# A hybrid decoder step on one core: matmul rows and split weights at other addresses modulo 256

## The chip, the core and the metric

The kernel runs on one core of a Trainium2 chip, as one program. The metric is the device time of one execution in microseconds (us), taken as the median of several. TensorE (PE) multiplies, PEld stands for its weight loads, VectorE (DVE), ScalarE (ACT) and GpSimd (POOL) do the elementwise work, and SyncE (SP) issues most of the DMAs.

## What is computed

One inference step of a two-layer decoder with 256 prompt tokens and 8 sequences of 4 new tokens, 288 tokens in all, of width 1024. Each layer is a mixer between two half-step SwiGLU FFNs. Cut to what matters here:

```python
def swiglu(x, w_gu, w_down):                       # w_gu 1024 x 5632, w_down 2816 x 1024
    g, u = jnp.split(x @ w_gu, 2, axis=-1)
    return (jax.nn.silu(g) * u) @ w_down

for i in range(2):
    x = x + 0.5 * swiglu(rmsnorm(x, norm_ffa[i]), w_ffa_gu[i], w_ffa_down[i])
    h = rmsnorm(x, norm_mix[i])
    x = x + (short_conv_mixer(h, ...) if i == 0 else nsa(h, ...))   # each with an input and an output projection
    x = x + 0.5 * swiglu(rmsnorm(x, norm_ffb[i]), w_ffb_gu[i], w_ffb_down[i])
y = rmsnorm(x, norm_final)
```

All weights and activations are fp32. The attention mixer (nsa) reads a compressed, a selected and a windowed cache.

## The kernel before

Activations lie transposed: channels on the 128 partitions, the 288 tokens along the row. A weight matrix comes in chunks of up to 1 MB from HBM (Weights.load_ahead, L209) into a ring of four buffers, raw. A unit is half a chunk: up to 8 blocks of 128 x 128. Each unit is split into two fp32r parts: ScalarE writes the rounded part, whi (L242), VectorE the remainder, wlo = raw - whi (L251). Both lie in the pool split, four buffers of 4096 bytes per partition for each name, all of whi first and then all of wlo. Activations are split in the same way into pairs of tiles: xh and xl hold the normed inputs (L395, L398), Ah and Al the products of gate and up, or of the convolution (L560, L561, L635, L636), and zh and zl the normed input of the last FFN.

A product of a unit is three matmuls for each of its blocks k (product; the profile shows them all at L307, in the helper mm): whi with xh, whi with xl, wlo with xh. The activations' row is the moving operand (288 columns), the weights' block is the one that is loaded (128 columns). All accumulate in one PSUM bank, which VectorE then empties. The code says in Python which engine does what in which order; the conversions of the next units stand between the products, two units ahead.

Each pair tile is made by rows(): row n begins at SKIP[name] + n x ROW fp32 words in the tile, where ROW is 320 words (1280 bytes, of which 1152 are used), and BEHIND adds unused words after the last row. The pool gives the tiles their places in the order in which they are first asked for, so SKIP, BEHIND and the sizes decide at which address modulo 256 the rows begin. As ROW is five times 256 bytes, all rows of a tile begin at the same address modulo 256, and so do all blocks of 512 bytes in a unit. In the program before these are:

| | whi | wlo | xh, Ah, zh | xl, Al, zl | raw |
|---|---|---|---|---|---|
| address modulo 256 | 64 | 64 | 64 | 128 | 64 |
| distance of a row from whi | | | 0 | 64 | |
| distance of a row from wlo | | | 0 | 64 | |

In the attention mixer the split ring's buffers hold pages of the cache for a while (L1030, load_pages). [...]

Of the kernel before, what the change touches and what calls it, by code (L numbers as in the profile page):

```python
# [8 lines left out]
F32 = mybir.dt.float32  # L9
F32R = mybir.dt.float32r  # L10
# [6 lines left out]
P = 128  # L17
# [49 lines left out]

V_FFA, V_PE, V_MIX, V_FFB, V_FIN, V_CONV = 0, 16, 32, 48, 64, 72

ROW = 320  # L70
SKIP = dict(xh=0, xl=16, Ah=56, Al=16, zh=56, zl=16)
BEHIND = dict(xl=8, zl=56)


def weight_chunks():

    steps = [range(k * P, (k + 1) * P) for k in range(NF)]

    def ffn(name, layer, first=False):
        for f0, f1 in HALVES:  # L80
            cuts = list(range(f0, f1, 2)) + [f1]
            if first and not f0:
                cuts = [f0] + list(range(f0 + 1, f1, 2)) + [f1]
            for f, e in zip(cuts, cuts[1:]):
                for c in (0, FF):
                    yield f"w_{name}_gu", layer, steps[:KD], [range(c + f * P, c + e * P)]
            m = (f1 - f0) // 2
            for d in range(0, KD, 2):
                for i in range(2):
                    yield f"w_{name}_down", layer, steps[f0 + i * m:f0 + (i + 1) * m], [range(d * P, (d + 2) * P)]  # L90

    yield from ffn("ffa", 0, True)
    for d in range(0, KD, 2):
        for part in (1, 2, 0):
            yield "w_conv_in", 0, steps[:KD], [range(part * D + d * P, part * D + (d + 2) * P)]
    for d in range(0, KD, 2):
        yield "w_conv_out", 0, steps[:KD], [range(d * P, (d + 2) * P)]
    yield from ffn("ffb", 0)
    yield from ffn("ffa", 1)
    for t in range(6):  # L100
        yield "w_nsa_in", 0, steps[:KD], [range(D + t * 256, D + (t + 1) * 256)]
    yield "w_nsa_in", 0, steps[:KD], [range(D + 6 * 256, N_IN)]
    for pr in range(2):
        for gp in range(2):
            yield "w_nsa_in", 0, steps[:KD], [range((2 * pr + kp) * 256 + gp * P, (2 * pr + kp) * 256 + (gp + 1) * P) for kp in range(2)]

    heads = [[r for kp in range(2) for r in range(((pr * 2 + kp) * 4 + g) * HD, ((pr * 2 + kp) * 4 + g + 1) * HD)]
             for pr in range(2) for g in range(4)]
    for d in range(0, KD, 2):
        yield "w_nsa_out", 0, heads, [range(d * P, (d + 2) * P)]  # L110
    yield from ffn("ffb", 1)


class Task:


    def __init__(self, engine, takes, put, after=(), slots=(), uses=(), rank=0.0):
        self.engine, self.takes, self.put, self.after, self.slots, self.rank = engine, takes, put, after, slots, rank
        self.end = None
        for x in (*slots, *uses):  # L120
            x.users.append(self)
# [53 lines left out]
class Weights:  # L175
# [5 lines left out]
    def __init__(self, nc, raw, split, bufs, given):  # L181
        self.given, self.at, self.plan = given, dict.fromkeys(given, 0), weight_chunks()
        self.nc, self.raw, self.split, self.bufs = nc, raw, split, bufs
        self.chunks, self.units = [], []
        self.loaded = self.done = self.used = 0
        self.live = 0
        self.left = {}
        self.tiles, self.parts, self.halves = {}, {}, {}
        self.stop = None
        self.behind = None  # L190

    def chunk(self):

# [27 lines left out]
    def low_behind(self):  # L221
# [2 lines left out]
            self.low(n)  # L224
        self.behind = []

    def high(self):
        c, view = self.units[self.done]
        v = view(self.tiles[c])
        hi, lo = [self.split.tile([P, 1024], F32R, name=n) for n in ("whi", "wlo")]  # L230
        n = 1
        for x in v.shape[1:]:
            n *= x
        parts = []
        for t in (hi, lo):
            t = t[:, :n]
            if len(v.shape) == 4:
                t = t.rearrange("p (k a c) -> p k a c", a=v.shape[2], c=v.shape[3])
            else:
                t = t.rearrange("p (k c) -> p k c", c=v.shape[2])  # L240
            parts.append(t)
        self.nc.scalar.activation(parts[0], v, AF.Copy)  # L242
        nk = v.shape[1]
        self.halves[self.done] = c, v, parts
        self.parts[self.done] = [t[:, :n].rearrange("p (k c) -> p k c", k=nk) for t in (hi, lo)]
        self.done += 1
        return self.done - 1
# [28 lines left out]
def tile_step(ctx, tc, x_turned, vectors, state_turned, cmp_pages, sel_pages, cache_win, win_pages, page_table,  # L276
# [3 lines left out]
    nc = tc.nc  # L280
    const = ctx.enter_context(tc.tile_pool(name="const", bufs=1))
    raw = ctx.enter_context(tc.tile_pool(name="raw", bufs=RAW))
    split = ctx.enter_context(tc.tile_pool(name="split", bufs=SPLIT))
# [52 lines left out]
    def tr(out, in_):  # L336
# [4 lines left out]
    W = Weights(nc, raw, split, RAW, dict(  # L341
        w_ffa_gu=w_ffa_gu, w_ffa_down=w_ffa_down, w_ffb_gu=w_ffb_gu, w_ffb_down=w_ffb_down, w_conv_in=w_conv_in,
        w_conv_out=w_conv_out, w_nsa_in=w_nsa_in, w_nsa_out=w_nsa_out))
# [41 lines left out]
    def rows(pool, name, n, **k):  # L385

        t = pool.tile([P, SKIP[name] + n * ROW + BEHIND.get(name, 0)], F32R, name=name, **k)
        return t[:, SKIP[name]:][:, :n * ROW].rearrange("p (n c) -> p n c", c=ROW)[:, :, :N]

    xh, xl = rows(const, "xh", KD), rows(const, "xl", KD)  # L390
# [143 lines left out]
    def pair(work, name, n):  # L534
        return [rows(work, name + part, n, bufs=1) for part in "hl"]
# [300 lines left out]
    def nsa(at):  # L836
# [167 lines left out]
        def load_chunk(tiles, b, j):  # L1004

            vs = [t.rearrange("p (s c) -> p s c", c=512) for t in tiles]
            if j != "w":
                at_ = page_numbers(b * 16 + j * 4, 4)
            s0 = 0
            for v in vs:  # L1010
                m = v.shape[1]
                if j == "w":
                    nc.sync.dma_start(v, win_pages[4 * b + s0:4 * b + s0 + m].rearrange("s p c -> p s c"))
                else:
                    for s in range(m):
                        nc.sync.dma_start(v[:, s:s + 1], sel_pages[bass.ds(at_[s0 + s], 1)].rearrange("s p c -> p s c"))
                s0 += m
            return vs

        def load_pages():  # L1020
            while len(pages) + len(done) < len(order):
                n = len(pages) + len(done)
                ring = max(room, key=lambda r: room[r] if r != "split" or n < PAGES["until"] else 0)
                if not room[ring] or ring == "split" and n >= PAGES["until"]:
                    return
                i, j, b2 = key = order[len(pages) + len(done)]
                b = 2 * i + b2
                room[ring] -= 1
                if ring == "split":
                    t = [split.tile([P, 1024], F32R, name=n).bitcast(F32) for n in ("whi", "wlo")]  # L1030
                else:
                    t = [(raw if ring == "raw" else early).tile([P, 2048], F32, name=ring)]
                pages[key] = load_chunk(t, b, j)
                rings[key] = ring
            W.stop, W.bufs = None, room["raw"]
            W.load_ahead()
# [106 lines left out]
        def load_more(at):  # L1143
            n = len(pages) + len(done) + W.loaded - W.attention
            load_pages()
            for k in range(n, min(len(pages) + len(done) + W.loaded - W.attention, len(loads))):
                queue[0] = max(queue[0], at) + LOAD
                loads[k].end = queue[0] + LAND
# [36 lines left out]
        x = Slot("tr")  # L1185
# [103 lines left out]
        def sequences(i):  # L1289
# [34 lines left out]
            def best():  # L1324

                left, kept = [T(n, [P, 34]) for n in ("left", "kept")]
                nc.vector.tensor_reduce(sc[:, 1:31], t["rank"][:, 2:62].rearrange("p (n r) -> p n r", r=2), AX.X, OP.add)
                high = T("top", [P, 8])
                for src_, dst in ((sc, left), (left, kept)):
                    nc.vector.max(high, src_[:, 0:33])  # L1330
                    nc.vector.match_replace(dst[:, 0:33], high, src_[:, 0:33], NEG)
                t["mk"] = T("mk", [P, 32], F32, 2)
                ts(t["mk"], kept[:, 0:32], 0.0, NEG, op0=OP.is_ge, op1=OP.mult)
# [288 lines left out]
```

## Time and profile before

| | us |
|---|---|
| median of 3 runs | 1236.58 (1236.1 to 1237.55) |
| the profiled execution | 1236.77 |
| its span, first to last instruction | 1235.0 |
| PE busy in the span | 1218.2 (99%) |
| PEld busy | 1153.3 (93%) |
| DVE busy | 730.3 (59%) |
| ACT busy | 571.1 (46%) |
| POOL busy | 236.8 (19%) |

The mean granted TensorE clock is 0.997 of full speed. DMA moves 262 MB, 212 GB/s over the span. In the profile a busy time counts each engine's instructions; matmuls overlap in the pipeline, so that their durations are longer than the distance between their starts. A group line gives a line of the kernel, engine, operation, output and inputs, shapes, count, then busy us and mean ns of one, then the idle time before them and what ended it.

### The profile page before, as it was taken

Reading aid. Unit: us, or ns where it says so; the run is one execution under the profiler, and the core shown is the slowest. Engines: PE = TensorE matmul, PEld = TensorE weight load, DVE = VectorE, ACT = ScalarE, POOL = GpSimd, SP = SyncE. Lnnn points to the kernel's source line nnn. Section 1 sums busy time; section 2 is a strip of 40 time slices with the busy share of each in tenths; the row PEclk is TensorE's granted clock in tenths of the full one; section 3 lists DMA queues with packets and bytes.
Section 4 is the critical chain, followed back from the end, with each engine's and each line's share of the span. In section 5 each row is a group of like instructions: output and inputs, shape, how many; then the busy total and the mean of one; then the engine's idle time right before and its main releaser. Section 6 shows DMA issues by size and latency. Waiting matters only on the chain.

```text
span 1235.0 us, 25757 instructions
## 1 busy us (share of the span) xinstructions
PE 1218.2 (99%) x10047; PEld 1153.3 (93%) x10047; DVE 730.3 (59%) x1363; ACT 571.1 (46%) x1011; POOL 236.8 (19%) x237
## 2 busy tenths in 40 slices
PE   9999999999999999999999999999999999999997
PEld 8999999999999999999899999999866699999997
DVE  6663555666765545556564455676568566655654
ACT  6443344533544334345443344544377645443444
POOL 0260121231321101212120012130022222200211
PEclk9999999999999999999999999999999999999999
DMA  7764655756566466546573453596699857575532
GB/s 280 262 219 174 235 175 185 256 188 221 189 217 211 155 211 236 195 152 237 198 238 119 174 178 113 175 344 211 238 366 332 294 206 282 211 254 205 165 102 80
DMA packets 89066, 262.00 MB, mean 212 GB/s; under 512 B 9937, under 2 KB 43090, under 8 KB 73714
## 3 DMA queue, kind: packets, MB, share of 16 engines
q1 hardware_dynamic: 87922, 249.66, 57.6%
q0 software_dynamic: 256, 8.32, 1.8%
q10 hardware_dynamic: 768, 2.38, 0.5%
q8 instruction: 79, 1.29, 0.4%
q14 instruction: 41, 0.34, 0.1%
HBM read 257.31 MB, written 11.35 MB: 218 GB/s over the span
## 4 chain that ended last, share of the span: by engine, by line
PE 92%; ACT 3%; DVE 3%; DMA 2%; issue 1%; POOL 0%; SPq 0%; DVEq 0%; ACTq 0%
PE mm L307 83%; PE tr L307 5%; PE acc L307 3%; PE tr L338 1%; DMA early<-in_sel_pages_dram 1%; ACT S L1219 1%; DVE wlo L251 1%; DMA raw<-in_w_nsa_out_dram 0%; ACT L542 0%; ACT whi L242 0%; DMA raw<-in_w_ffa_gu_dram 0%; DVE xT L591 0%; ACT S L1375 0%; DVE S L1371 0%; ACT sq L404 0%
## 5 line engine op out<-in xcount | busy, mean ns | idle before, releaser
L251 DVE TENSOR_TENSOR wlo<-raw,whi 128x1024 fp32r<-128x1024 f32 (+2 forms) x361 | 411.9, 1155 | 93.4 <-ACT whi L242 91.1
L307 PE MATMUL mm<-xh,whi 128*128 128x288 f32 (+1 forms) x1480 | 436.5, 297 | 2.5 <-DVE xl L1484 1.1
L307 PE MATMUL mm<-xl,whi 128*128 128x288 f32 (+1 forms) x1480 | 432.4, 294 | 0.0
L307 PE MATMUL mm<-xh,wlo 128*128 128x288 f32 (+1 forms) x1480 | 428.7, 292 | 0.0
L242 ACT ACTIVATE whi<-raw 128x1024 fp32r<-128x1024 f32 (+2 forms) x365 | 343.2, 952 | 97.5 <-PE mm L307 86.1
L307 PEld LDWEIGHTS mm<-xh,whi 128*128 128x128 f32 (+1 forms) x1480 | 276.8, 188 | 7.9 <-issue 3.8
L307 PEld LDWEIGHTS mm<-xl,whi 128*128 128x128 f32 (+1 forms) x1480 | 277.0, 188 | 0.5 <-DVE xl L398 0.2
L307 PEld LDWEIGHTS mm<-xh,wlo 128*128 128x128 f32 (+1 forms) x1480 | 276.0, 187 | 0.4 <-DVE wlo L251 0.2
L307 PE MATMUL mm<-Ah,whi 128*128 128x288 f32 x768 | 226.4, 295 | 0.0
L307 PE MATMUL mm<-Ah,wlo 128*128 128x288 f32 x768 | 224.9, 293 | 1.3 <-DVE wlo L251 1.1
L307 PE MATMUL mm<-Al,whi 128*128 128x288 f32 x768 | 225.4, 294 | 0.0
L557 POOL TENSOR_TENSOR a<-s,t 128x288 f32<-128x288 f32 x80 | 104.8, 1310 | 514.9 <-DVE t L555 376.4
L307 PEld LDWEIGHTS mm<-Ah,wlo 128*128 128x128 f32 x768 | 144.2, 188 | 2.7 <-DVE wlo L251 2.7
L307 PEld LDWEIGHTS mm<-Ah,whi 128*128 128x128 f32 x768 | 144.0, 188 | 0.7 <-issue 0.4
L307 PEld LDWEIGHTS mm<-Al,whi 128*128 128x128 f32 x768 | 144.0, 188 | 0.0
L553 ACT ACTIVATE s<-t 128x288 f32<-128x288 f32 x88 | 39.1, 445 | 159.2 <-DVE t L551 159.1
L560 ACT ACTIVATE Ah<-a 128x288 fp32r<-128x288 f32 x88 | 39.1, 445 | 154.4 <-POOL a L557 141.7
L555 DVE TENSOR_TENSOR t<-mm,rB 128x288 f32<-128x288 f32 x88 | 40.2, 457 | 111.8 <-PE mm L307 111.6
L307 PE MATMUL mm<-zh,whi 128*128 128x288 f32 x352 | 103.5, 294 | 0.0
L307 PE MATMUL mm<-zl,whi 128*128 128x288 f32 x352 | 103.3, 294 | 0.0
L307 PE MATMUL mm<-zh,wlo 128*128 128x288 f32 x352 | 102.8, 292 | 0.0
L591 DVE SCALAR_TENSOR_TENSOR xT<-mm,xT 128x288 f32<-128x288 f32 x64 | 29.2, 456 | 86.1 <-PE mm L307 85.6
(291 smaller groups left out, 1173.4 us busy)
## 6 DMA issues: line engine op xcount, KB each, us to landing
raw<-in_w_ffb_gu_dram SPq DMA_DIRECT2D x44, 1024.0 KB, 5.1
raw<-in_w_ffa_gu_dram SPq DMA_DIRECT2D x42, 1024.0 KB, 5.4
cp<-in_cmp_pages_dram SPq DMA_DIRECT2D x256, 128.0 KB, 4.4
early<-in_sel_pages_dram SPq DMA_DIRECT2D x56, 256.0 KB, 5.4
raw<-in_w_ffa_down_dram SPq DMA_DIRECT2D x16, 768.0 KB, 4.6
raw<-in_w_conv_in_dram SPq DMA_DIRECT2D x12, 1024.0 KB, 5.0
raw<-in_w_ffb_down_dram SPq DMA_DIRECT2D x16, 768.0 KB, 5.6
raw<-in_sel_pages_dram SPq DMA_DIRECT2D x48, 256.0 KB, 5.1
```

Source lines behind the costliest of these rows:

```text
L242: self.nc.scalar.activation(parts[0], v, AF.Copy)
L251: (lower or self.nc.vector).tensor_sub(parts[1], v, parts[0])
L307: nc.tensor.matmul(out, lhsT, rhs, start=start, stop=stop, skip_group_check=True)
L338: nc.tensor.transpose(out, in_, ident[:k, :k])
L553: nc.scalar.activation(s1, t1, AF.Silu)
L555: nc.vector.tensor_mul(t2, pu[:, :N], rB)
L557: (nc.vector if last else nc.gpsimd).tensor_mul(a, s1, t2)
L560: nc.scalar.activation(Ah[:, f], a, AF.Copy)
L591: nc.vector.scalar_tensor_tensor(xT[:, d], py[:, :N], 0.5, xT[:, d], op0=OP.mult, op1=OP.add)
L1219: nc.scalar.activation(o, o, AF.Exp, scale=-1.0, bias=x, accum_out=e)
```

## The change

The constants of rows() are others: SKIP is now 7 words (28 bytes) for xh, 39 (156) for xl, Al and zl, 63 (252) for Ah and zh; BEHIND becomes 25 for xl and 24 for zl. A new method, Weights.pair, allocates whi and wlo and puts a tile of 16 words (64 bytes), gap, between the two rings once; high and load_pages call it in place of their own two allocations. The room for POOL's DMA descriptors goes from 16,384 to 1024 bytes per partition, which moves all tiles down by 15,360 bytes. No instruction is added, taken away or moved, with their shapes as before.

```diff
-ROW = 320
-SKIP = dict(xh=0, xl=16, Ah=56, Al=16, zh=56, zl=16)
-BEHIND = dict(xl=8, zl=56)
+ROW, GAP = 320, 16
+SKIP = dict(xh=7, xl=39, Ah=63, Al=39, zh=63, zl=39)
+BEHIND = dict(xl=25, zl=24)
...
+    def pair(self):
+        hi = self.split.tile([P, 1024], F32R, name="whi")
+        if self.gap is None:
+            self.gap = self.split.tile([P, GAP], F32, name="gap", bufs=1)
+        return [hi, self.split.tile([P, 1024], F32R, name="wlo")]
+
     def high(self):
         c, view = self.units[self.done]
         v = view(self.tiles[c])
-        hi, lo = [self.split.tile([P, 1024], F32R, name=n) for n in ("whi", "wlo")]
+        hi, lo = self.pair()
...
-                    t = [split.tile([P, 1024], F32R, name=n).bitcast(F32) for n in ("whi", "wlo")]
+                    t = [x.bitcast(F32) for x in W.pair()]
...
-    nc = bacc.Bacc("TRN2", target_bir_lowering=False, num_devices=1)
+    nc = bacc.Bacc("TRN2", target_bir_lowering=False, num_devices=1, dynamic_dma_scratch_size=1024)
```

In the program built from it the addresses are:

| | whi | wlo | xh, Ah, zh | xl, Al, zl | raw |
|---|---|---|---|---|---|
| address modulo 256 | 0 | 64 | 92 | 252 | 0 |
| distance of a row from whi | | | 92 | 252 | |
| distance of a row from wlo | | | 28 | 188 | |

More of the change, by code (lines that the diff above doesn't have):

```diff
@@ L189, in __init__ @@
         self.stop = None
-        self.behind = None
+        self.behind = self.gap = None
     def chunk(self):
```

## The prediction

> **What bounds the kernel now.** I read the busy table, the clock and the chain on the page first, then the costliest groups, then the order of time on TensorE and its weight loader.
>
> ```profile
> span 1235.0 us, 25757 instructions
> PE 1218.2 (99%) x10047; PEld 1153.3 (93%) x10047; DVE 730.3 (59%) x1363; ACT 571.1 (46%) x1011; POOL 236.8 (19%) x237
> PEclk9999999999999999999999999999999999999999
> PE 92%; ACT 3%; DVE 3%; DMA 2%; issue 1%; POOL 0%; SPq 0%; DVEq 0%; ACTq 0%
> PE mm L307 83%; PE tr L307 5%; PE acc L307 3%; PE tr L338 1%; DMA early<-in_sel_pages_dram 1%; ACT S L1219 1%; DVE wlo L251 1%; DMA raw<-in_w_nsa_out_dram 0%; ACT L542 0%; ACT whi L242 0%; DMA raw<-in_w_ffa_gu_dram 0%; DVE xT L591 0%; ACT S L1375 0%; DVE S L1371 0%; ACT sq L404 0%
> ```
>
> The chain that ends last is TensorE for 92% of the span and the projections' matmuls (mm, L307) for 83%, at the full granted clock. A busy PE is not a PE at its peak, so the question is how close together these matmuls start. There are nine groups of them:
>
> ```profile
> L307 PE MATMUL mm<-xh,whi 128*128 128x288 f32 (+1 forms) x1480 | 436.5, 297 | 2.5 <-DVE xl L1484 1.1
> L307 PE MATMUL mm<-xl,whi 128*128 128x288 f32 (+1 forms) x1480 | 432.4, 294 | 0.0
> L307 PE MATMUL mm<-xh,wlo 128*128 128x288 f32 (+1 forms) x1480 | 428.7, 292 | 0.0
> L307 PE MATMUL mm<-Ah,whi 128*128 128x288 f32 x768 | 226.4, 295 | 0.0
> L307 PE MATMUL mm<-Ah,wlo 128*128 128x288 f32 x768 | 224.9, 293 | 1.3 <-DVE wlo L251 1.1
> L307 PE MATMUL mm<-Al,whi 128*128 128x288 f32 x768 | 225.4, 294 | 0.0
> L307 PE MATMUL mm<-zh,whi 128*128 128x288 f32 x352 | 103.5, 294 | 0.0
> L307 PE MATMUL mm<-zl,whi 128*128 128x288 f32 x352 | 103.3, 294 | 0.0
> L307 PE MATMUL mm<-zh,wlo 128*128 128x288 f32 x352 | 102.8, 292 | 0.0
> ```
>
> The counts add up to 3 x (1480 + 768 + 352) = 7800. A mean of 292 to 297 ns each would be 2.28 ms in a row, almost twice the span, so these durations overlap. The spacing of the starts is what counts. In the order of time, inside the first FFN (start in us, duration in us, engine, instruction):
>
> ```profile
> 59.84 0.29 PE L307 MATMUL mm<-xh,whi 128*128 128x288 f32 x1
> 59.97 0.29 PE L307 MATMUL mm<-xl,whi 128*128 128x288 f32 x1
> 60.09 0.30 PE L307 MATMUL mm<-xh,wlo 128*128 128x288 f32 x1
> 60.23 0.29 PE L307 MATMUL mm<-xh,whi 128*128 128x288 f32 x1
> ...
> 66.00 0.30 PE L307 MATMUL mm<-xh,wlo 128*128 128x288 f32 x1
> ```
>
> From 59.84 to 66.00 us there are 48 starts, all listed without an idle time: 6.16 us / 47 = 131.1 ns from one to the next. So 7800 x 131.1 ns = 1022.6 us, 83% of the span, the chain's own share. The weight loads beside them:
>
> ```profile
> 59.84 0.19 PEld L307 LDWEIGHTS mm<-xl,whi 128*128 128x128 f32 x1
> 59.97 0.19 PEld L307 LDWEIGHTS mm<-xh,wlo 128*128 128x128 f32 x1
> 60.10 0.19 PEld L307 LDWEIGHTS mm<-xh,whi 128*128 128x128 f32 x1
> ```
>
> The load for the next matmul starts when the current matmul starts. So while TensorE streams a row of xh it reads whi for xl, while it streams xl it reads wlo, and while it streams xh a second time it reads the next whi. Two streams of reads leave the same partitions at the same time, at addresses that have a fixed distance modulo 256, because a row is 1280 bytes (five times 256) and a weight block 512.
>
> What would 288 columns take with no disturbance? The nearest row is the plain fp32 product in the token factor, near 17.5 us:
>
> ```profile
> 17.54 0.65 PE L307 MATMUL acc<-ss,ones 128*128 128x288 f32 x2
> L307 PE MATMUL acc<-ss,ones x12: 403/406/407, 17.5 to 1021.5; 128*128 128x288 f32 x12
> ```
>
> Two passes last 0.65 us together and 406 ns each, so the second started 0.65 - 0.406 = 0.244 us after the first. If those passes stream at half the speed of the fp32r ones, as the factor of about two suggests, 288 columns alone take 122 ns, and the 131.1 ns hold about 9 ns that is not streaming. That is an estimate. Over 7800 matmuls it is 7800 x 9 = 70 us, the most that an edit of addresses can give. [...]
>
> **The change, part by part.** Every instruction stays: same operations, sizes, engines and order. No step of the sum is an instruction more or less. Only addresses move.
>
> *Distances between the two read streams.* Before, modulo 256, a row of xh begins 0 bytes from whi and from wlo, a row of xl 64 from both (Ah, zh and Al, zl likewise). Afterwards xh begins 92 bytes from whi and 28 from wlo, xl 252 from whi and 188 from wlo. By pairs that read together: xh with whi goes from 0 to 92, xl with wlo from 64 to 188. New, too, is that all rows begin 12 bytes past a multiple of 16, while before all began on a multiple of 64. No matmul of this speed in the trace has such a distance, so no row prices it and I bound it. Below: all of the 9 ns goes, 70 us. Above: the single starts quoted lie 130, 120 and 140 ns apart; if 140 ns (the printed longest, to 10 ns) became the rule, 7800 x 8.9 = 69 us more. That the spacing is uneven, while all operands have the same size, is the sign that something beside streaming sets it. That the nine groups' means differ by 5 ns at most, though some stand at distance 0 and some at 64, says that whole multiples of 64 change little. [...]
>
> I take a third of the 9 ns: 3 ns, nearer to no change than to the floor, since the two distances that the trace does show lie so close together. 7800 x 3 ns = 23.4 us. Of this, about 95% reaches the end: the chain is PE for 92%, and at the few waits of TensorE for the vector or scalar engine an earlier TensorE only waits longer. That is 22 us. What is late next? A gate*up chunk serves 48 matmuls, 48 x 128.1 = 6.15 us, and its load lands in less, with four raw buffers:
>
> ```profile
> raw<-in_w_ffb_gu_dram SPq DMA_DIRECT2D x44, 1024.0 KB, 5.1
> L251 DVE TENSOR_TENSOR wlo<-raw,whi 128x1024 fp32r<-128x1024 f32 (+2 forms) x361 | 411.9, 1155 | 93.4 <-ACT whi L242 91.1
> L242 ACT ACTIVATE whi<-raw 128x1024 fp32r<-128x1024 f32 (+2 forms) x365 | 343.2, 952 | 97.5 <-PE mm L307 86.1
> ```
>
> One unit of 24 matmuls takes 3.07 us and needs one whi (952 ns) and one wlo (1155 ns), so neither engine becomes the bound.
>
> *Vector and scalar work on the moved rows.* The engines that write xh, xl, Ah and Al do it at the odd starts, and whi and raw begin elsewhere:
>
> ```profile
> L561 DVE TENSOR_TENSOR Al<-a,Ah 128x288 fp32r<-128x288 f32 x88 | 41.1, 468 | 59.0 <-ACT Ah L560 59.0
> L398 DVE SCALAR_TENSOR_TENSOR xl<-xT,vecT,xh 128x288 fp32r<-128x288 f32 x40 | 26.3, 670 | 15.7 <-ACT xh L395 15.7
> ```
>
> 67.4 us of busy time together. A tenth more would be 7 us, on an engine 59% busy and on the chain for 3%, so 0.2 us at the end. Nothing; without that cover, at the ends of the FFNs, it would cost 0.05 to 0.07 us for each row.
>
> *The smaller ring for descriptors of POOL's DMAs.* It is used eight times:
>
> ```profile
> L1562 POOL DMA_DIRECT2D out_dram<-in_cache_win_kv_dram x8: 488/547/682, 1019.6 to 1087.4; - x8
> DMA to landing us min/median/max: 5.6/6.9/8.2
> ...
> 1086.83 1.03 POOL L1562 DMA_DIRECT2D out_dram<-in_cache_win_kv_dram  x2
> ```
>
> The first six go out over 67 us, some 11 us apart, with landings after at most 8.2 us, so one has landed before the next. The last two go out together; if the second had to wait, POOL's next multiply (a, L557) would start up to 8.2 us late, at 1087 us, where the chunk it makes is not read until the down products. I take nothing, and 8 us at most.
>
> Sum: the profiled execution took 1236.77 us (its span of 1235.0 and 1.8 around it), 0.2 above the median of 1236.58. 1236.6 - 22 = 1214.6, forecast 1214 us.
>
> **The rivals.**
>
> *The address makes no difference (12%).* Then the 9 ns belong to the handover from one matmul to the next, and the time stays 1236.6. For it: the groups at distance 0 and at 64 differ little. Against it: starts of equal matmuls 120 to 140 ns apart. [...]
>
> *Slower: rows that straddle (22%).* If the array fetches in aligned pieces of four words, a row of 1152 bytes on an aligned start covers 72 of them; begun 12 bytes into a piece it covers 73. If each piece costs its share of the time, a matmul takes 131.1 / 72 = 1.8 ns more: 7800 x 1.8 = 14 us, 1250.8 us. It happens on every one of the 7800, and it decides if the shift within a piece wins less than 1.8 ns from the meeting of the two streams; with meetings made more frequent besides, the 140 ns above is the limit. For it: nothing is read less, and something more. [...]
>
> *Nearly all of the 9 ns goes (part of the faster case).* Then 7800 x 9 x 0.95 = 67 us, 1170 us. For it, the fp32 pair at 244 ns shows that 288 columns can run beside a weight load of 128 at the streaming time alone. Against it, at half speed two streams have twice the room.
>
> **How the numbers follow.** A measurement of this kernel can tell 0.2% from no change, 2.5 us: below 1234.1 is faster, above 1239.1 slower. Faster 66%, the forecast and its larger variant: from 1170 to 1233, centred on 1214. The same 12%. Slower 22%: mostly about 1251, with a tail to 1275. The range 1180 to 1252 leaves out the last tenth of the full gain (about 8%) and the tail above the straddling price (about 10%). Since cases of both signs stand in it, the likeliest one's own range is 1180 to 1230.
>
> **What would show it.** If I am right, starts of mm in the same stretch lie about 128 ns apart (48 in 6.02 us), the count of 7800 and the durations of wlo and whi stay, and the idle times before PE hardly grow. If they lie at 131 ns, the address doesn't matter; at 133 ns, the straddling rival holds; at 123 ns, all of the excess was the meeting of the two streams. The forecast is wrong in its reasoning, even at the right time, if the gain stands in waits of TensorE and not in the spacing, or if only one of the three kinds of matmul moved.

## The result and the profile after

The changed kernel takes 1223.31 us (median of 4 runs, 1221.45 to 1225.61), the kernel before 1236.78 us beside it (1236.1 to 1237.55). The ratio is 0.9892, 95% interval 0.9873 to 0.9911: 13.5 us faster, where 22 were forecast. The profiled execution took 1222.47 us. The page of the changed kernel, busy times, clock and chain:

```profile
span 1220.7 us, 25758 instructions
PE 1203.6 (99%) x10047; PEld 1138.3 (93%) x10047; DVE 728.4 (60%) x1363; ACT 570.3 (47%) x1011; POOL 238.3 (20%) x237
PEclk9999999999999999999999999999999999999999
PE 87%; DVE 4%; ACT 4%; issue 1%; DMA 1%; SPq 1%; POOL 0%; DVEq 0%; ACTq 0%; POOLq 0%
```

The span is 14.3 us shorter, PE's busy time 14.6 and its weight loader's 15.0; what the span has beside PE's busy time is 16.8 us before and 17.1 afterwards. The count of matmuls is the same, and the busy times of VectorE, ScalarE and GpSimd have hardly moved. In the order of time, at the same place of the first FFN as before (start, duration, instruction; the line of mm is now L313):

```profile
59.72 0.29 PE L313 MATMUL mm<-xh,wlo 128*128 128x288 f32 x1
59.85 0.29 PE L313 MATMUL mm<-xh,whi 128*128 128x288 f32 x1
59.98 0.29 PE L313 MATMUL mm<-xl,whi 128*128 128x288 f32 x1
60.11 0.29 PE L313 MATMUL mm<-xh,wlo 128*128 128x288 f32 x1
60.24 0.29 PE L313 MATMUL mm<-xh,whi 128*128 128x288 f32 x1
60.37 0.29 PE L313 MATMUL mm<-xl,whi 128*128 128x288 f32 x1
...
65.93 0.29 PE L313 MATMUL mm<-xh,wlo 128*128 128x288 f32 x1
```

From 59.72 to 65.93 us there are 49 starts: 6.21 / 48 = 129.4 ns, where it was 131.1. The starts are also even now: 45 of the 48 distances are 130 ns by the printed hundredths and three are 120, where 120, 130 and 140 stood before. That the whole trace moved in this way is seen from a mean that is used in all that follows, the **spacing**: over the 7800 projection matmuls, by the trace's time stamps in ns, the distance from one start to the next where no other matmul stands between, without the distances over 170 ns (85 before, 76 afterwards). A high row is one of xh, Ah or zh, a low row one of xl, Al or zl; the three kinds of matmul are the high row with whi, the low row with whi and the high row with wlo. Before it is 131.24 ns over 7670 pairs, afterwards 129.47 over 7679. The difference of 1.77 ns times 7800 is 13.8 us of the span's 14.3. By kind: the start after a matmul of the high row with whi went from 131.4 to 129.6, after the low row with whi from 132.0 to 129.6, after the high row with wlo from 130.4 to 129.2. The gain is in the spacing, in all three kinds, and not in waits.

The other lines that the prediction leaned on, in the changed kernel (groups of VectorE and ScalarE, the loads of a chunk, the eight DMAs of POOL):

```profile
L257 DVE TENSOR_TENSOR wlo<-raw,whi 128x1024 fp32r<-128x1024 f32 (+2 forms) x361 | 409.9, 1149 | 96.9 <-ACT whi L248 94.3
L248 ACT ACTIVATE whi<-raw 128x1024 fp32r<-128x1024 f32 (+2 forms) x365 | 342.6, 950 | 95.0 <-PE mm L313 62.4
L567 DVE TENSOR_TENSOR Al<-a,Ah 128x288 fp32r<-128x288 f32 x88 | 41.2, 468 | 59.1 <-ACT Ah L566 59.1
L404 DVE SCALAR_TENSOR_TENSOR xl<-xT,vecT,xh 128x288 fp32r<-128x288 f32 x40 | 26.7, 680 | 15.9 <-ACT xh L401 15.9
raw<-in_w_ffb_gu_dram SPq DMA_DIRECT2D x44, 1024.0 KB, 5.2
L1568 POOL DMA_DIRECT2D out_dram<-in_cache_win_kv_dram x8: 488/550/682, 1007.7 to 1074.7; - x8
DMA to landing us min/median/max: 5.5/6.4/8.5
```

VectorE's and ScalarE's work on rows at odd starts takes what it took (Al 468 ns in both, xl 680 in place of 670; ScalarE's Ah 444 in place of 445, xh 534 in both), and the first six DMAs with the smaller ring go out 11.2 to 13.5 us apart, where it was 11.3 to 13.6.

### The profile page after: what moved, and what is told of

Read it like the earlier page. It is cut to its first block, busy times and chain, and to the rows that moved or that the text cites. A ratio compares the mean times of both kernels' runs of the same rounds, so it can differ in the third digit from the quotient of the medians.

```text
span 1220.7 us, 25758 instructions
## 1 busy us (share of the span) xinstructions
PE 1203.6 (99%) x10047; PEld 1138.3 (93%) x10047; DVE 728.4 (60%) x1363; ACT 570.3 (47%) x1011; POOL 238.3 (20%) x237
## 4 chain that ended last, share of the span: by engine, by line
PE 87%; DVE 4%; ACT 4%; issue 1%; DMA 1%; SPq 1%; POOL 0%; DVEq 0%; ACTq 0%; POOLq 0%
PE mm L313 78%; PE tr L313 5%; PE acc L313 3%; DVE wlo L257 2%; PE tr L344 1%; ACT whi L248 1%; ACT S L1225 1%; SPq L1022 1%; ACT sq L410 1%; DMA raw<-in_w_nsa_out_dram 0%; DMA early<-in_sel_pages_dram 0%; ACT L548 0%; DVE xT L597 0%; DMA raw<-in_w_ffa_gu_dram 0%; ACT PTs L1390 0%
## 5 line engine op out<-in xcount | busy, mean ns | idle before, releaser
L313 PE MATMUL mm<-xh,whi 128*128 128x288 f32 (+1 forms) x1480 | 432.0, 294 | 2.5 <-DVE xl L1490 1.1
L313 PE MATMUL mm<-xl,whi 128*128 128x288 f32 (+1 forms) x1480 | 427.6, 291 | 0.0
L313 PE MATMUL mm<-xh,wlo 128*128 128x288 f32 (+1 forms) x1480 | 426.3, 291 | 0.0
L313 PEld LDWEIGHTS mm<-xh,whi 128*128 128x128 f32 (+1 forms) x1480 | 275.7, 187 | 7.9 <-issue 3.0
L313 PEld LDWEIGHTS mm<-xl,whi 128*128 128x128 f32 (+1 forms) x1480 | 275.7, 187 | 0.5 <-DVE xl L404 0.2
L313 PEld LDWEIGHTS mm<-xh,wlo 128*128 128x128 f32 (+1 forms) x1480 | 275.4, 187 | 0.6 <-DVE wlo L257 0.5
L313 PE MATMUL mm<-Ah,wlo 128*128 128x288 f32 x768 | 223.6, 291 | 1.8 <-DVE wlo L257 1.8
L313 PE MATMUL mm<-Ah,whi 128*128 128x288 f32 x768 | 224.4, 292 | 0.0
L313 PE MATMUL mm<-Al,whi 128*128 128x288 f32 x768 | 223.3, 291 | 0.0
L313 PEld LDWEIGHTS mm<-Ah,wlo 128*128 128x128 f32 x768 | 143.9, 187 | 3.2 <-DVE wlo L257 3.2
L313 PEld LDWEIGHTS mm<-Ah,whi 128*128 128x128 f32 x768 | 143.8, 187 | 0.8 <-issue 0.4
L313 PEld LDWEIGHTS mm<-Al,whi 128*128 128x128 f32 x768 | 143.8, 187 | 0.0
L313 PE MATMUL mm<-zh,wlo 128*128 128x288 f32 x352 | 102.3, 291 | 0.3 <-DVE wlo L257 0.3
L313 PE MATMUL mm<-zh,whi 128*128 128x288 f32 x352 | 102.6, 291 | 0.0
L313 PE MATMUL mm<-zl,whi 128*128 128x288 f32 x352 | 102.3, 291 | 0.0
```

The lines of the kernel that those rows point to most:

```text
L313: nc.tensor.matmul(out, lhsT, rhs, start=start, stop=stop, skip_group_check=True)
```

## The experiments

Each kernel differs from the changed one by the edit shown. Distances are those of a row from whi modulo 256, high row and low row; where no gap is named, wlo stands like whi. Where a kernel has its own SKIP, BEHIND fills each tile up to a multiple of 256 bytes; Bh and Bl in it are the starts of Ah and Al in the last FFN.

### Is it the place, or the smaller ring? (place_only)

```diff
-SKIP = dict(xh=7, xl=39, Ah=63, Al=39, zh=63, zl=39)
+SKIP = dict(xh=40, xl=56, Ah=56, Al=8, zh=56, zl=8)      # 0 and 64, as before
-        if self.gap is None:
-            self.gap = self.split.tile([P, GAP], F32, name="gap", bufs=1)
```

> The smaller descriptor ring and the lower place of all tiles as in the changed kernel, but the rows' distances from the split weights as before: 0 for xh, Ah, zh and 64 for xl, Al, zl, no gap between the rings. Theory (the meeting of the two read streams, set by the distances): 1236 to 1237 us, starts 131.1 ns apart. Rival (the place in SBUF or the smaller ring brings the gain): 1223 us, starts 129.4 ns apart.

Measured: 1236.26 us against 1236.47, ratio 1.0002 (0.9991 to 1.0014), spacing 131.2 ns. The theory holds: the lower place and the ring of 1024 bytes do nothing. In the program built from this kernel whi stands at 224 modulo 256, in the kernel before at 64: rows and weights moved together leave the spacing alone.

### The 12 bytes alone, and the steps of 16 alone (only_12, whole_16)

```diff
+SKIP = dict(xh=43, xl=59, Ah=59, Al=11, zh=59, zl=11)    # only_12: 12 and 76, no gap
```

> The distances of before plus 12 bytes each: 12 for xh, Ah, zh and 76 for xl, Al, zl, from whi and wlo alike, no gap. Theory (the 12 bytes count): 1222 to 1225 us, starts 129 ns apart. Rival (the distance in steps of 16 counts): 1235 to 1238 us, starts 131 ns apart. If rows that straddle cost something by themselves: above 1237 us.

Measured: 1235.78 us against 1236.47, ratio 0.9995 (0.9986 to 1.0005), spacing 131.1 ns. The theory falls: beside the distances of before, the 12 bytes bring nothing. They cost nothing either.

```diff
+SKIP = dict(xh=60, xl=36, Ah=60, Al=36, zh=60, zl=36)    # whole_16: 80 and 240, with the gap
```

> The changed kernel with every row begun 12 bytes earlier: distances 80 and 240 from whi, 16 and 176 from wlo, all multiples of 16. Theory (the 12 bytes count): the gain goes, 1235 to 1238 us, and the starts are uneven again. Rival (the distance in steps of 16 counts): 1222 to 1225 us, even starts.

Measured: 1246.06 us against 1236.47, ratio 1.0082 (1.0065 to 1.0099), spacing 132.5 ns: slower than before the change. The same 12 bytes are worth 3 ns here and nothing there. Neither theory holds as it was put: the whole distance counts, and the fraction of 16 as well.

### The gap (no_gap)

```diff
+SKIP = dict(xh=63, xl=39, Ah=15, Al=55, zh=15, zl=55)    # 92 and 252
-        if self.gap is None:
-            self.gap = self.split.tile([P, GAP], F32, name="gap", bufs=1)
```

> The changed kernel without the gap of 64 bytes: rows 92 and 252 bytes from whi, and so 92 and 252 from wlo too. If only the pairs that read together count (a row of xl with the wlo block of the next matmul), just xl with wlo moves, from 188 to 252, and only the start after an xl matmul can change. Theory (the shift by 12 bytes beside a multiple of 16 is what counts): about 1223 us, as with the gap. Rival (the whole distance modulo 256 counts for each pair): the matmuls of xl with whi go back towards 132 ns, about 2600 x 2 ns = 5 us of the 13.5 lost, 1228 us.

Measured: 1228.23 us against 1236.47, ratio 0.9929 (0.9911 to 0.9947), spacing 130.0 ns. The start after a low row goes from 129.6 to 130.8, after a high row with whi from 129.6 to 130.0. The gap is worth some 0.5 ns a matmul, a third of the gain. Most of it stands in the start after the low row, beside which a block of wlo is loaded, and the time is the rival's 1228 us.

### The whole curve, row by row (sweep_low, sweep_high)

With ROW = 321 in place of 320, each row of a tile stands 4 bytes further, and one kernel shows 40 distances.

```diff
-ROW, GAP = 320, 16
+ROW = 321
+SKIP = dict(xh=40, xl=40, Ah=0, Al=0, zh=12, zl=12, Bh=20, Bl=20)      # sweep_high: 16, 40, 52, 60
...
+        skip = SKIP[name.replace("A", "B") if pool.name == "ffn1" else name]
+        size = skip + n * ROW
+        t = pool.tile([P, size + -size % 64], F32R, name=name, **k)
```

> Rows 1284 bytes apart in place of 1280, so that each row of a tile has its own distance, the same from whi and from wlo: xh and xl 0 to 28 bytes in steps of 4, Ah and Al of the first three FFNs 32 to 76, zh and zl 80 to 108, Ah and Al of the last FFN 112 to 156. The distance between starts is read row by row. Theory (the meeting of the two streams depends on the distance modulo 256): one curve, between 129 and 134 ns, low near 92, high near 80, about 131 at 0, 64 and 76. Rival (only the fraction of 16 bytes counts): the curve repeats every four rows. Rival (it is the combination of three different distances): flat within 1 ns.

> The other half of the same curve: xh and xl 160 to 188 bytes, Ah and Al of the first three FFNs 192 to 236, zh and zl 240 to 12, Ah and Al of the last FFN 16 to 60. Theory: the rows at 188 and at 252 are low (129.5 to 131 ns), 176 and 240 higher, 131 at 12; the rows of the last FFN at 16 to 28 and 32 to 60 agree with the other tiles' at the same distances in the first half, within 1 ns. Rivals as there.

Measured: 1252.13 us against 1237.17 (one run each) and 1250.78 against the same, mean spacing 133.4 and 133.1 ns. Sorted by the place of the row's start within 16 bytes, 20 rows of distances each, the spacing has these means: on a multiple of 16, 132.0 ns (129.2 to 134.6); 4 bytes in, 135.5 (133.4 to 145.7); 8 bytes in, 134.2 (130.8 to 136.0); 12 bytes in, 131.8 (129.9 to 134.1). So the place within 16 counts for 2 to 4 ns, and within each class the rows spread over 4 ns or more. It is neither the one curve between 129 and 134 ns of the theory, nor a repeat every four rows, nor flat. Of the 16 distances at which two pairs of tiles stood, 10 agreed within a ns (24 bytes: 134.75 in both; 28: 130.4 and 130.5), five within 1.4, and one not (16: 134.6 and 131.3): what a matmul takes depends on its neighbours too.

### Is it the load beside the row? (half_load)

Half of the output rows get no correction by the low parts here, so that two weight loads of three take half the columns.

```diff
+            c = min(64, hi.shape[2])                          # on place_only
-            mm(o, hi[:, k], al[:, k0 + k], False, False)
-            mm(o, lo[:, k], ah[:, k0 + k], False, e)
+            mm(o[:c], hi[:, k, :c], al[:, k0 + k], False, False)
+            mm(o[:c], lo[:, k, :c], ah[:, k0 + k], False, e)
```

> The kernel of place_only (distances 0 and 64), where in the products of one unit after another the matmuls of xl with whi and of xh with wlo take 64 of the 128 weight columns: half of the output rows get no correction by the low parts. Two loads of three last half as long, each matmul still streams 288 columns. Theory (about 9 ns of the 131 are the meeting of the row's reads with the load's): the starts after the two matmuls that read beside a short load lie 126 to 127 ns apart, the third kind stays near 131; 7000 matmuls, two thirds of them 4 to 5 ns less: about 21 us, 1215 us. Rival (a fixed cost of the handover from one matmul to the next): all stay near 131 ns, 1236 us.

Measured: 1237.94 us against 1237.17, spacing 131.4 ns, by kinds (high row with whi, low with whi, high with wlo) 132.1, 131.8 and 130.4, where place_only has 131.5, 131.9 and 130.2. The weight loader of this kernel in the order of time, and the first and last of the 48 starts of matmuls in this stretch:

```profile
60.33 0.19 PEld L311 LDWEIGHTS mm<-xh,whi 128*128 128x128 f32 x1
60.47 0.14 PEld L311 LDWEIGHTS mm<-xl,whi 128*64 128x64 f32 x1
60.60 0.14 PEld L311 LDWEIGHTS mm<-xh,wlo 128*64 128x64 f32 x1
60.73 0.19 PEld L311 LDWEIGHTS mm<-xh,whi 128*128 128x128 f32 x1
```

```profile
59.81 0.29 PE L311 MATMUL mm<-xl,whi 128*64 128x288 f32 x1
...
65.97 0.29 PE L311 MATMUL mm<-xh,whi 128*128 128x288 f32 x1
```

The loads last 0.14 us in place of 0.19, which is three quarters and not half, and the matmuls still start 6.16 / 47 = 131.1 ns apart. The theory of the prediction, that the spacing above the streaming time is the meeting of the row's reads with the load's, falls in the form that it had: by it, half of the columns and three quarters of the load's time had to bring the starts after a short load closer together, and they stand at 132.1 and 131.8 ns, where place_only has 131.5 and 131.9.

### Shorter rows and still shorter loads (short_and_tiny)

Beside what half_load leaves out, the last 96 tokens get no low correction in the products of xh and xl, and three quarters of the output rows get none in those of Ah, Al and zh, zl.

```diff
+            if ah is xh:
+                t = 192
+            elif nk > 4:
+                c = 32
+            mm(o[:c, :t], hi[:, k, :c], al[:, k0 + k, :t], False, False)
```

> The kernel of half_load with two more things left out. Where xh and xl are multiplied, the xl matmul streams 192 of the 288 columns (the last 96 tokens get no such correction); where Ah, Al or zh, zl are multiplied, the low matmuls take 32 weight columns in place of 64. Theory now, after half_load (a fixed cost at each handover, on which the addresses put 1 to 3 ns): the start after a row of 192 columns comes 132 - 40 = 92 ns later (96 columns at 0.417 ns, half of the fp32 rate), and loads of 32 columns change nothing: 131 ns. Rival A (the row itself streams slower than the estimate, by its share): 131.8 x 192 / 288 = 88 ns. Rival B (the meeting with the load after all, in the load's first part): with loads of 32 columns the spacing falls to 127 ns or below. Time 1173 to 1180 us.

Measured: 1189.76 us against 1234.52, above the 1173 to 1180 expected. Loads of 32 columns, in the down products (loader, then matmuls, in the order of time):

```profile
106.44 0.19 PEld L311 LDWEIGHTS mm<-Ah,whi 128*128 128x128 f32 x1
106.57 0.11 PEld L311 LDWEIGHTS mm<-Al,whi 128*32 128x32 f32 x1
106.71 0.11 PEld L311 LDWEIGHTS mm<-Ah,wlo 128*32 128x32 f32 x1
```

```profile
106.57 0.30 PE L311 MATMUL mm<-Ah,whi 128*128 128x288 f32 x1
106.71 0.29 PE L311 MATMUL mm<-Al,whi 128*32 128x288 f32 x1
106.84 0.29 PE L311 MATMUL mm<-Ah,wlo 128*32 128x288 f32 x1
106.97 0.29 PE L311 MATMUL mm<-Ah,whi 128*128 128x288 f32 x1
```

Three starts still take 106.97 - 106.57 = 0.40 us; over all of Ah and Al of the first three FFNs the kinds are at 130.5, 132.1 and 134.2 ns, 132.3 in the mean. Rival B falls with that: loads of 0.11 us in place of 0.19 bring no matmul closer to the next. They aren't without effect, as the start after a high row with wlo comes 4 ns later than in place_only (130.1 there). With rows of 192 columns (lines from the first FFN; the means below are over all such rows of xh and xl):

```profile
60.05 0.29 PE L311 MATMUL mm<-xh,whi 128*128 128x288 f32 x1
60.19 0.25 PE L311 MATMUL mm<-xl,whi 128*64 128x192 f32 x1
60.27 0.30 PE L311 MATMUL mm<-xh,wlo 128*64 128x288 f32 x1
60.41 0.29 PE L311 MATMUL mm<-xh,whi 128*128 128x288 f32 x1
```

The short row is followed 87.7 ns later in the mean, as rival A had it, but its two neighbours have grown, from 132.2 to 133.1 and from 130.2 to 132.5 ns. A triple takes 353.3 ns in place of 394.1: 40.8 ns for 96 columns, 0.425 a column, which is nearer to the 40 of a fixed cost at each handover than to the 44 of a slower stream. No run shows the 0.417 ns a column that the 40 comes from; half of the fp32 pair's 0.244 us over 288 columns is 0.424, and by the trace's time stamps (242 ns) 0.420, so that the estimate is 40 to 41. The two neighbours' growth, 0.9 and 2.3 ns, is as large as the difference of 3; so this run doesn't decide between the two.

### The parts of the change by themselves (parts_mixed, parts_mixed_2)

Each pair of tiles gets its own distances, so that one kernel holds four combinations, with rows 1280 bytes apart and the gap. In the kernels in which all pairs stand alike, the pairs agree within 0.4 ns, so that they can be compared.

```diff
+SKIP = dict(xh=63, xl=56, Ah=40, Al=39, zh=40, zl=56, Bh=63, Bl=39)
```

> With the gap of 64 bytes between the rings, four pairs of tiles stand at four combinations of distances from whi: xh, xl at 92, 64 (only the xh part of the change); Ah, Al of the first three FFNs at 0, 252 (only the xl part); zh, zl at 0, 64 (only the gap); Ah, Al of the last FFN at 92, 252 (the change as it is). Theory (each pair of reads counts for itself, by distance modulo 256): the last FFN shows 129.4 ns as in the changed kernel, and each part alone gives some of the 1.8 ns: the first two lie between 129.4 and 131.2 ns, the gap alone at 131. Rival (only the combination counts): each part alone at 131 ns or above. Time about 1230 us, each of the combinations with its own spacing.

Measured: 1704.61 us at a granted clock of 0.654 for the whole execution, which no other run showed; nothing is read from it.

> The kernel of parts_mixed once more, since TensorE's granted clock was 0.654 in that execution and its spacings say nothing. With the gap: xh, xl at 92, 64; Ah, Al of the first three FFNs at 0, 252; zh, zl at 0, 64; Ah, Al of the last FFN at 92, 252. Theory now (a row that begins 12 bytes into 16 streams up to 2 ns faster than one that begins on 16, for 288 columns, and the other distances add half a ns): the last FFN 129.4 ns; of x the two xh matmuls near 130 and the xl one near 132, of A the other way round; z 131 to 132. Rival (only the combination counts): x and A at 131 to 132 in all three kinds.

Measured: 1233.17 us against 1236.25. With the gap, the high rows' move alone (92, 64) stands at 130.1 ns, the low rows' alone (0, 252) at 132.2, the gap by itself (0, 64) at 131.8, all three (92, 252) at 129.5. By kinds of x (129.7, 130.4, 130.1 for high with whi, low, high with wlo) the start after the untouched low row improved as well, and after the moved low row of A it did not (132.4): the kinds don't answer one by one, as the theory had it, and x at 130 in all three kinds is not what the rival had. The high rows carry the change. The gap, by itself or with the low rows' move, brings nothing (131.8 and 132.2 ns against 131.2); the gap and the low rows' move each bring some 0.5 ns beside the other two edits. The high rows' move and the low rows', each by itself without the gap, were not run. The change's combination gives 129.5 ns here with whi at 224 modulo 256, as in the changed kernel with whi at 0: the distances count, not the place.

### Are the low points of the curve good for all rows? (lows_steady)

```diff
+SKIP = dict(xh=56, xl=56, Ah=52, Al=52, zh=35, zl=35, Bh=63, Bl=63)    # 64, 240, 172, 28, no gap
```

> No gap, rows 1280 bytes apart again; each pair of tiles stands at one of the lowest distances of the two sweeps, the same for both tiles and both rings: xh, xl at 64, Ah, Al of the first three FFNs at 240, zh, zl at 172, Ah, Al of the last FFN at 28. Theory (the distance of the row in hand sets the spacing, whatever row came before): 129.2, 129.5, 129.9 and 130.5 ns as in the sweeps, within 0.5 ns; about 1222 us. Rival (the neighbouring rows of the sweep made them low): 131 to 132 ns, about 1238 us.

Measured: 1238.29 us against 1234.52. 64 stands at 132.0 and 240 at 132.1 ns, 2.6 to 2.7 more than in the sweep; 172 and 28, which begin 12 bytes past a multiple of 16, at 130.0 both. The time is the rival's. The low points on multiples of 16 were the neighbours' doing, as it had it; those at 12 bytes hold within 0.5 ns.

### Word by word around the change (steps_of_4)

```diff
+SKIP = dict(xh=61, xl=37, Ah=62, Al=38, zh=0, zl=40, Bh=63, Bl=39)     # with the gap
```

> The change's three distances (92, 252 and the gap) moved along together by words, one shift for each pair of tiles, rows 1280 bytes apart: xh, xl 8 bytes earlier (84, 244: 4 bytes into a piece of 16); Ah, Al of the first three FFNs 4 bytes earlier (88, 248: 8 into it); zh, zl 4 bytes later (96, 256: on a piece); Ah, Al of the last FFN as in the change (92, 252: 12 into it); whole_16 was 12 bytes earlier (132.5 ns). Theory now (the place of the row's start within 16 bytes sets how fast the row streams): 84 and 88 at 134 to 136 ns, 96 at 131 to 132, 92 at 129.5; 1480 x 3 x 5 + 588 x 3 x 5 = 31 us above the changed kernel, about 1255 us. Rival (a smooth optimum around 92): 88 and 96 within 1 ns of 129.5, 84 near 131.

Measured: 1267.74 us against 1236.43. The spacings are 136.2 ns (8 bytes before the change's place), 135.5 (4 before), 129.5 (the change's own), 135.5 (4 behind). Matmuls of the first pair, 47 starts, and of the pair at the change's place, 49 starts:

```profile
59.70 0.30 PE L312 MATMUL mm<-xh,whi 128*128 128x288 f32 x1
...
65.98 0.30 PE L312 MATMUL mm<-xl,whi 128*128 128x288 f32 x1
```

```profile
1149.74 0.29 PE L312 MATMUL mm<-Al,whi 128*128 128x288 f32 x1
...
1155.96 0.29 PE L312 MATMUL mm<-Al,whi 128*128 128x288 f32 x1
```

6.28 / 46 = 136.5 ns and 6.22 / 48 = 129.6 ns in one and the same execution; in the changed kernel, where both pairs have the same distances, they stand at 129.5 ns both, so that the address of the rows makes the difference. A smooth optimum falls; one word to either side costs 6 ns. The theory of steps_of_4 holds for 92 and, within 1.5 ns, for 84 and 88, and falls at 96, a multiple of 16, which it had at 131 to 132 ns; the time is above its 1255 us. Time and spacing agree: (135.5 - 131.2) x 7800 = 33.5 us, and the run is 31.3 us above the kernel before.

## Why the prediction was right, and where it was not

**The place of the gain.** The forecast put it in the spacing of the 7800 projection matmuls and in nothing else. That is what the two traces show: 13.8 of 14.3 us, in all three kinds and not in waits.

**The size.** The term "3 ns of 9" measured 1.77. This term is mis-sized, and the step below it is why it could not be sized: 70 us as the most that addresses can give rests on a floor of 122 ns that no kernel's mean here came near. That the fp32 pair's 0.244 us are streaming alone, and that an fp32r matmul streams in half of it, was the author's estimate, which no run shows. The lowest spacing where all rows of a tile stand alike is the change's own 129.5; no row of the sweeps is below 129.2 in the mean of its kinds.

**The mechanism.** The step "two streams of reads leave the same partitions at the same time" as the cause of the 9 ns is the one that failed, as far as shorter loads can show it. Loads of half and a quarter of the columns (0.14 and 0.11 us in place of 0.19) leave the spacing at 131.4 and 132.3 ns. What the runs put in its place: the spacing is set by where the rows begin, within 16 bytes and modulo 256, and no simple rule for it came out. These are the combinations that were run with all rows of a tile at the same distance.

| start within 16 bytes | distances from whi, high and low row | gap | spacing, ns | run |
|---|---|---|---|---|
| 12 | 92, 252 (the change) | yes | 129.5 | the changed kernel |
| 12 | 92, 252 | no | 130.0 | no_gap |
| 12 | 28, 28 | no | 130.0 | lows_steady |
| 12 | 172, 172 | no | 130.0 | lows_steady |
| 12 | 12, 76 | no | 131.1 | only_12 |
| 12 and 0 | 92, 64 | yes | 130.1 | parts_mixed_2 |
| 0 and 12 | 0, 252 | yes | 132.2 | parts_mixed_2 |
| 0 | 0, 64 (before) | no | 131.2 | the kernel before, place_only |
| 0 | 0, 64 | yes | 131.8 | parts_mixed_2 |
| 0 | 64, 64 | no | 132.0 | lows_steady |
| 0 | 240, 240 | no | 132.1 | lows_steady |
| 0 | 80, 240 | yes | 132.5 | whole_16 |
| 0 | 96, 256 | yes | 135.5 | steps_of_4 |
| 8 | 88, 248 | yes | 135.5 | steps_of_4 |
| 4 | 84, 244 | yes | 136.2 | steps_of_4 |

The weights' place has a part in it (the gap, 0.5 ns; rows and weights moved together change nothing), but loads of half or a quarter of the columns bring nothing. Whether the first reads of a load matter, those of fewer than 32 columns, was not tried. The rival that the address makes no difference falls with the 129.5 to 136.2 ns of the table.

**Luck.** That the time fell was luck in part. The step that was to make it fall is the one that failed, and of the 13 other combinations in the table eight are slower than the kernel before. Nothing in the prediction's working picks 92 and 252 with the gap from among them.

**"Whole multiples of 64 change little"** was read from the distances 0 and 64, which the kernel before had beside each other (131 to 132 ns). It held for 64 throughout (132.0); other multiples of 16 reach from 132.1 to 135.5.

**"New, too, is that all rows begin 12 bytes past a multiple of 16"** was half right as a cause. Starts at 12 bytes are the best class in the first sweep (131.7 ns against 132.2 on multiples of 16) and level with these in the second (131.8 and 131.7); going from the change to 80 and 240 loses 3 ns; but only_12 gains nothing. The kernel before stood at the best of the combinations on multiples of 16 in the table.

**The straddling rival** had each start off a multiple of 16 pay for a 73rd piece, 1.8 ns. Pieces of four words were the rival's assumption, and no run shows them; what the sweeps show is that their means differ by the place within 16 bytes. Starts 4 and 8 bytes in pay 2 to 4 ns (135.5 and 134.2 against 132.0), those 12 bytes in would touch 73 pieces as well and pay nothing in the mean (131.8). A price for the one piece more is not borne out.

**The edits at nothing** were that: place and ring 1.0002 (0.9991 to 1.0014), Al 468 ns in both. The prediction read the gaps of POOL's DMAs too wide: 67 us is the stretch of all eight, and the first six go out over 61.2 us, 11.3 to 13.6 apart, still longer than a landing (8.2 at most). The 95% that were to arrive can't be told from all: 13.8 us of spacing stand beside 14.3 of the span and 13.5 of the medians. The chain went from PE 92% to 87%, with splits of weights in more of it (wlo 2% and whi 1%, where they had 1% and 0%), but PE's share of the span stayed at 99%.

**Still open:** why 12 bytes into 16, and why one combination of three distances is 3 to 7 ns better than the same shifted by 4 to 12 bytes. In the programs built from these kernels whi and wlo begin on multiples of 32 bytes, so a row's place within 16 bytes and its distance from the weights within 16 bytes are the same number: whether the row's own place counts or its place against the weights', no run separates. short_and_tiny leaves undecided whether the time above the estimate is a cost of each handover or a slower stream.

## What to carry to other kernels

Where matmuls follow each other without waits, measure the distance of their starts over some fifty of them, not their durations, and look whether it is even: an uneven row of starts at equal sizes (120 to 140 ns by the printed hundredths, and 45 of 48 at 130 after the change) showed here that addresses had a say. The place of the moving rows moved a matmul of 288 columns by up to 7 ns of 130 (129.5 to 136.2), so try it on the chip a word at a time, in a kernel that gives each tile its own start, and then run the chosen one with all rows alike, because what a row shows here was not all its own (64 bytes from whi: 129.2 ns in the sweep, 132.0 with all rows of the tile alike). A floor worked out from another kind of matmul is not a price for an edit.

## What the runs showed of the hardware that was not expected

- Moving rows that begin 4 or 8 bytes past a multiple of 16 stand 2 to 4 ns above those on one in the sweeps' means (135.5 and 134.2 against 132.0 ns), and 6 to 7 ns above the change's rows where all rows of a tile stand alike (136.2 and 135.5 against 129.5). Rows that begin 12 bytes past it cost nothing in the mean (131.8), and in the best combination they save 1.8 ns (129.47 against 131.24).
- Weight loads of 64 or 32 columns in place of 128 do not bring matmuls of 288 columns closer together (131.4 and 132.3 ns against 131.2).
- At one distance of the sweep, 84 bytes for both rows, matmuls stood 145.7 ns apart in the mean; beside other rows and with the gap (84 and 244) it was 136.2.
- One execution of a one-core program ran at a granted clock of 0.654 from end to end (1704.61 us), the next of the same kernel, on another chip, at 0.997 (1233.17 us). Two other kernels of this study ran on the first chip at 0.997 and 0.998.
